# Output projection of a hybrid attention and Hyena layer: left half of the columns for all tokens, then the right half token group by token group

## The chip, the cores and the metric

One core of one Trainium2 chip runs the kernel. The metric is the device time of one execution in microseconds (us), here the median of three runs. The trace comes from one more, profiled execution; its span is counted from its first recorded instruction, and every time below is in us from there.

The engines go by the trace's names: PE is TensorE with its matmuls, ACT is ScalarE, DVE is VectorE, POOL is GpSimd, and SP is the queue that issues most transfers. Each engine works through its own list of instructions in order; an instruction that waits holds up all that stand behind it on that engine.

## What is computed

One layer: attention and a long convolution run side by side, are merged by gates into `y`, and go through one output projection `w_out` (1024 by 1024) into a gated residual. A norm, a router over 64 experts, the experts and a shared expert follow.

```python
def merge_branches(attn_out, hy_out, gate, w_ba, w_bh, w_out):
    ga, gh = jnp.split(gate, 2, axis=-1)
    y = jax.nn.sigmoid(ga) * (attn_out @ w_ba) + jax.nn.sigmoid(gh) * (hy_out @ w_bh)
    return y @ w_out
...
        x_mixed = x + mod[:, 2] * merge_branches(attn, hy_out, gate, w_branch_attn[i],
                                                 w_branch_hyena[i], w_out[i])
...
        x = x_mixed
        h2 = modulate(rmsnorm(x, norm_ffn[i]), mod[:, 3], mod[:, 4])
        x = x + mod[:, 5] * moe(h2, w_router[i], router_bias[i], w_exp_gate[i], w_exp_up[i],
                                w_exp_down[i], w_sh_gate[i], w_sh_up[i], w_sh_down[i])
    return rmsnorm(x, final_norm)
```

There are 512 tokens, in four groups of 128.

## The kernel before, in words

**Matmuls in pairs.** Every fp32 operand of a large matmul is kept as a pair: `hi`, the value cast to a shorter form, and `lo`, what the cast lost. `split` (L103) makes it from the raw weights: ACT casts `hi` (L105), then DVE, or POOL where the caller says so, subtracts it from the raw value (L106). `mm3` (L97) multiplies two pairs with three matmuls (hi·hi, hi·lo, lo·hi).

**Stages of the middle of the kernel.** Attention and Hyena come first. The merge (L872 to L895, eight steps `j`) multiplies by `wbh` and `wba` and leaves `yT`, the merged activations transposed. Then follows the output projection: `outproj(a2)` (L1038) makes both column halves (n = 0, 1, 512 columns each) of two of the four token groups, with four banks of PSUM, over eight slices `j` of the weights. It is called twice, with a2 = 0 and 1, and each call loads and splits all sixteen weight tiles `wo` of 256 KB again. A raw tile stays in one of 7 buffers ("rwb") until it is split; the pair stays in one of 3 ("wb") until its matmuls are done. For n = 0 the `lo` part is DVE's, for n = 1 POOL's. Into the second call the loads of the shared expert's weights are woven, 8 of `wsgu` (`sg`) and 4 of `wsd` (`sd`), with the same raw buffers and `lo` on POOL. In the trace `wo110` is a2 = 1, n = 1, j = 0, and a raw tile has an `r` in front (`rwo`, `rsg`, `rsd`; a group's line leaves numbers out).

**After the matmuls.** DVE multiplies a bank of PSUM by the gate (`to`, L1055) and adds it to the residual (`xt`, L1056). `norm2(a)` (L1058) is a chain over ACT and DVE: ACT squares and sums `xt` (L1062), ACT makes a root (`rs_s`, L136, with a table load before it), five small operations of DVE refine it (L137 to L141), and DVE makes `h` in two passes (L1064, L1065). `turn2(a)` (L1070) transposes `h` on PE in two halves (`px`); ACT copies each half (`h2T`) and casts it (`sx`), DVE subtracts. `logit2(a)` (L1082) multiplies by the router's weights (`plg`, 16 matmuls per group in the trace) and takes a sigmoid (`score`).

**Order.** The order between the stages is the program's for the pinned parts (matmuls, ACT's copies, the shared expert); a scheduler weaves the rest into each engine's list at build time. Before, groups 0 and 1 are normed, turned and routed between and inside the two calls; groups 2 and 3 are normed after the second. The block behind it multiplies the first half of the tokens for the shared expert (`pgsh`, 24 matmuls), turns and routes groups 2 and 3, multiplies the second half (`pgsh` again), and then runs the router and a loop of 64 experts (`pge`, `pxe`, `pye`).

## Time and profile before

| | us |
|---|---|
| median of three runs | 1380.72 |
| the three runs | 1378.25, 1381.03, 1380.72 |
| the profiled execution | 1378.4 |
| its span | 1376.6 |
| mean granted clock of TensorE in it, as a share of full | 0.971 |

The profiled execution lies 2.3 us under the median and 0.15 us over the fastest run; 1.8 us of it lie outside the span. In the span the merge ends and the output projection begins at 495.9 us, the last matmul of the projection ends at 555.2 us, the second half of the shared expert's first product starts at 577.5 us, and the experts run from 610 us on. A stretch is read by the engine that is busy through it, and where none is, by what ends each engine's waits.

### The profile page before, as it was taken

To read this page: it belongs to the slowest core of one execution; us is meant where nothing else is said; L and a number is where in the kernel's file an instruction comes from. 1 tells how busy PE (TensorE), PEld (TensorE's weight loads), DVE (VectorE), ACT (ScalarE), POOL (GpSimd) and SP (SyncE) were. 2 spreads that over 40 slices of the span, in tenths; PEclk is the share of its full clock that TensorE was granted. 3 is DMA by queue.
4 is the path that set the end of the run, shared out by engine and by line. 5 is a ranking of instruction groups with operands and counts; after the bars stand their busy time and mean duration, and the time that the engine had idled before them with its cause. 6 is when DMAs were issued, how large, how long until landed. Compare 5 with 4: busy or idle time off the path is not lost.

```text
span 1376.6 us, 19781 instructions
## 1 busy us (share of the span) xinstructions
PE 1295.7 (94%) x7074; PEld 1051.8 (76%) x7074; DVE 1068.4 (78%) x1637; ACT 880.6 (64%) x1313; POOL 248.6 (18%) x233
## 2 busy tenths in 40 slices
PE   5999999999999998899999999999999999999970
PEld 3687777777776786778888888888888888888750
DVE  3678678986665549668888898988988898889855
ACT  5565554334664346437777877778877787777851
POOL 0000000002242458320111111111111111111120
PEclk8899999999999999899999999999999999999995
DMA  9433556554212647638999999899999999999944
GB/s 332 187 115 134 180 187 227 180 180 146 86 32 93 213 164 237 254 132 288 335 305 328 337 306 305 282 320 329 321 315 325 321 328 320 312 302 302 322 109 177
DMA packets 77063, 332.80 MB, mean 242 GB/s; under 512 B 13763, under 2 KB 15315, under 8 KB 47524
## 3 DMA queue, kind: packets, MB, share of 16 engines
q1 hardware_dynamic: 63460, 305.19, 61.6%
q0 software_dynamic: 11200, 22.14, 8.5%
q10 hardware_dynamic: 2304, 4.20, 0.8%
q8 instruction: 56, 0.92, 0.3%
q14 instruction: 43, 0.35, 0.1%
HBM read 296.91 MB, written 52.97 MB: 254 GB/s over the span
## 4 chain that ended last, share of the span: by engine, by line
PE 57%; DVE 4%; DMA 3%; issue 1%; ACT 1%; DVEq 0%; POOLq 0%; SPq 0%
PE pge L92 26%; PE pye L92 12%; PE pxe L1174 5%; PE pxe L1175 4%; DMA accd<-Ye,ixe 2%; PE pout L92 2%; PE pbh L92 2%; PE pba L92 2%; DMA accd<-Ys,ixs 1%; PE pgsh L92 1%; PE pte L95 1%; PE pysh L92 1%; PE sle L92 1%; DVE h L1065 0%; PE plg L92 0%
## 5 line engine op out<-in xcount | busy, mean ns | idle before, releaser
L1035 POOL DMA_INDIRECT accd<-Ye,ixe x64 | 106.1, 1658 | 607.1 <-ACT Ye L1034 386.3
L1174 PE MATMUL pxe<-oge,h2h 128*128 128x256 f32 x512 | 133.2, 293 | 0.2 <-DVE XTe00l L106 0.2
L1175 PE MATMUL pxe<-oge,h2l 128*128 128x256 f32 x512 | 128.6, 283 | 0.0
L1175 PEld LDWEIGHTS pxe<-oge,h2l 128*128 128x128 f32 x512 | 97.7, 191 | 3.2
L1174 PEld LDWEIGHTS pxe<-oge,h2h 128*128 128x128 f32 x512 | 97.6, 191 | 3.3 <-issue 0.6
L1034 ACT COPY Ye<-pye 128x1024 f32<-128x1024 f32 x64 | 65.1, 1017 | 9.1 <-PE pye L92 6.0
L779 DVE TENSOR_REDUCE st<-S 128x1 f32<-128x768 f32 x32 | 30.5, 956 | 22.7 <-PE S L92 22.0
L1007 ACT ACTIVATE aae<-pge 128x256 f32<-128x256 f32 x64 | 24.8, 387 | 32.4 <-PE pge L92 31.9
L783 ACT ACTIVATE P<-S,st 128x768 f32<-128x768 f32 x32 | 28.9, 903 | 11.9 <-DVE st L779 9.0
L1155 DVE TENSOR_TENSOR oge<-iot,posm 128x256 fp32r<-128x256 f32 x64 | 23.8, 420 | 13.4 <-PE pxe L1175 13.3
L1008 DVE SCALAR_TENSOR_TENSOR aae<-aae,wge,pge 128x256 f32<-128x256 f32 x64 | 30.5, 477 | 0.4
L800 PE MATMUL pT<-ident,P 128*128 128x128 f32 x192 | 29.9, 278 | 0.4 <-ACT PT L801 0.2
L547 POOL DMA_DIRECT2D modd<-br x16 | 7.9, 496 | 121.5 <-DVE br L546 121.5
L92 PE MATMUL po<-PT,V 128*64 128x256 f32 x192 | 29.1, 389 | 0.0
L800 PEld LDWEIGHTS pT<-ident,P 128*128 128x128 f32 x192 | 21.5, 140 | 7.5 <-issue 3.9
L92 PEld LDWEIGHTS sle<-R,oge 128*64 128x64 f32 x256 | 23.5, 137 | 4.2
L801 DVE COPY PT<-pT 128x384 f32<-128x384 f32 x32 | 17.6, 551 | 11.5 <-PE pT L800 11.4
L801 ACT COPY PT<-pT 128x384 f32<-128x384 f32 x32 | 15.3, 478 | 14.9 <-PE pT L800 14.7
L95 PE MATMUL pte<-ident,aae 128*128 128x128 f32 x128 | 24.4, 272 | 0.0
L311 POOL DMA_DIRECT2D specd<-fX x4 | 2.5, 615 | 120.9 <-DVE rl L301 120.1
L92 PE MATMUL pm<-wm,sc 128*32 128x256 f32 x128 | 13.8, 566 | 11.1 <-DMA wm<-in_wmod_dram 11.0
L92 PE MATMUL pgsh<-shguh,sx 128*128 128x512 f32 x64 | 23.8, 440 | 0.0
(6914 smaller groups left out, 4720.1 us busy)
## 6 DMA issues: line engine op xcount, KB each, us to landing
gu0e<-in_wgu_dram SPq DMA_DIRECT2D x64, 1024.0 KB
gu1e<-in_wgu_dram SPq DMA_DIRECT2D x64, 1024.0 KB
de<-in_wd_dram SPq DMA_DIRECT2D x64, 1024.0 KB
wn<-in_wmod_dram SPq DMA_DIRECT2D x16, 1024.0 KB
wm<-in_wmod_dram SPq DMA_DIRECT2D x16, 512.0 KB
rg<-in_win_dram SPq DMA_DIRECT2D x32, 256.0 KB
rwo<-in_wout_dram SPq DMA_DIRECT2D x32, 256.0 KB
rhy<-in_win_dram SPq DMA_DIRECT2D x24, 256.0 KB
```

Source lines behind the costliest of these rows:

```text
L92: pin(pe.matmul(o, lhsT, rhs, start=start, stop=stop))
L95: pin(pe.transpose(o, i, idn))
L779: dve.tensor_reduce(st[:, 0:1], S[:, 0:NKEY], AX.X, ALU.max, negate=True)
L783: act.activation(P, S[:, 0:NKEY], AF.Exp, bias=st[:, 0:1], accum_out=rsum[a][:, h % 2:h % 2 + 1])
L800: pe.transpose(pT[:, i * 128:(i + 1) * 128], P[:, kt * 128:(kt + 1) * 128], ident)
L801: (dve.tensor_copy if k3 else act.copy)(PT[:, 3 * k3:3 * k3 + 3, aa * 128:(aa + 1) * 128], pT.rearrange("p (k q) -> p k q", k=3))
L1007: pin(act.activation(self.aa, pg[:, 0:FF], AF.Silu))
L1008: dve.scalar_tensor_tensor(self.aa, self.aa, self.wg, pg[:, FF:], ALU.mult, ALU.mult)
L1034: act.copy(Y, py)
L1035: gp.indirect_dma_start(out=accd, out_offset=bass.IndirectOffsetOnAxis(ap=self.ix, axis=0), in_=Y, in_offset=None, compute_op=ALU.add, bou ...
L1174: pe.matmul(o, h2h[:, a, js], oh, start=(a % 2 == 0), stop=False)
L1175: pe.matmul(o, h2l[a][:, js], oh, start=False, stop=(a % 2 == 1))
```

## The change

The projection is cut in two others. `outproj_left` makes the left half of the columns for all four token groups at once, in four banks, with each left weight tile loaded and split once. `outproj_right(a)` makes the right half for one token group from eight pairs that stay in place: three in "wb", five in a new pool with tag "wo", through which the left tiles j >= 3 pass too. There are 16 weight loads in place of 32, 16 casts in place of 32, and 16 subtractions, all on DVE, in place of 16 on DVE and 16 on POOL. The number of matmuls stays. To make room, the raw buffers go from 7 to 5, and the gates `gt` of the merge get a pool of their own that is closed before the new pool opens.

The twelve loads of the shared expert stand in two calls of `shared_load` between the norms; half of the `sg` subtractions are now DVE's. The norms, turns and logits come one token group at a time between the right halves. The lists of all five engines are the same as before up to the merge, and again from the transposes of groups 2 and 3 on.

```diff
@@ -862,10 +862,13 @@
+    gst = ExitStack()
+    gtp = gst.enter_context(tc.tile_pool(name="gt", bufs=3, reuse_waits="tile"))
+
-    def gload(src, shape, name, dst=None, lo_eng=None):
-        raw = gpl.tile(shape, F32, name="r" + name, tag="rwb", bufs=7)
+    def gload(src, shape, name, dst=None, lo_eng=None, pool=None):
+        raw = gpl.tile(shape, F32, name="r" + name, tag="rwb", bufs=5)
         sp.dma_start(raw, src)
-        p = dst or pair(gpl, shape, name, "wb", 3)
+        p = dst or (pair(gpl, shape, name, "wb", 3) if pool is None else pair(pool, shape, name, "wo", 5))
         split(p[0], p[1], raw, lo_eng=lo_eng)
         return p
...
-        gt = gpl.tile([128, 2, T], F32, name=f"gt{j}", tag="gt", bufs=3)
+        gt = gtp.tile([128, 2, T], F32, name=f"gt{j}", tag="gt")
...
+    gst.close()
+    opl = mgs.enter_context(tc.tile_pool(name="op", bufs=1, reuse_waits="tile"))
...
+    def wout_load(n, j):
+        return gload(wout[n, :, j], [128, 512], f"wo{n}{j}", pool=opl if j >= 3 else None)
...
+    def outproj_left():
+
+
+        po = [bank(f"pout{a}0") for a in range(NA)]
         for j in range(8):
...
+            w = wout_load(0, j)
+            for a in range(NA):
+                mm3(po[a], at(yT, slice(None), j, slice(a * 128, a * 128 + 128)), w, j == 0, j == 7)
+            if j >= 2:
+                wo1.append(wout_load(1, j - 2))
+        for j in (6, 7):
+            wo1.append(wout_load(1, j))
+        for a in range(NA):
+            residual(po[a], a, 0)
+
+    def outproj_right(a):
+
+        po = bank(f"pout{a}1")
+        for j in range(8):
+            mm3(po, at(yT, slice(None), j, slice(a * 128, a * 128 + 128)), wo1[j], j == 0, j == 7)
+        residual(po, a, 1)
+
+    def shared_load(js):
+        for j in js:
+            gload(wsgu[:, j], [128, 512], f"sg{j}", at(shgu, slice(None), j), gp if j % 2 else None)
+        for f in range(2):
+            if len(js) == 4 and js[0] == 4:
+                for m in range(2):
                     cs = slice(m * 512, m * 512 + 512)
...
+                    gload(wsd[:, f, cs], [128, 512], f"sd{f}{m}", at(shd, slice(None), f, cs), gp)
...
-    outproj(0)
-    for a in range(2):
-        norm2(a)
-        turn2(a)
-    for a in range(2):
-        logit2(a)
-    outproj(1)
+    outproj_left()
+    outproj_right(0)
+    norm2(0)
+    shared_load(range(0, 4))
+    outproj_right(1)
+    turn2(0)
+    norm2(1)
+    shared_load(range(4, 8))
+    outproj_right(2)
+    logit2(0)
+    turn2(1)
     norm2(2)
+    outproj_right(3)
+    logit2(1)
     norm2(3)
     mgs.close()
     ps_open(ctx, y2=1, pg=2, pt=1)
```

On ACT, at the first norm: before, the sum of squares of group 0 (L1062) stands among the casts of `outproj(1)`, with nine of the shared expert's twelve casts behind it.

```order
L105 CAST wo110h_5251<-rwo110_5249 128x512
L105 CAST wo101h_5267<-rwo101_5265 128x512
L105 CAST shguh_4929<-rsg2_5311 128x512
L105 CAST wo111h_5279<-rwo111_5277 128x512
L1062 ACTIVATE h20_4913,ms20_5141<-xt0_3399 128x1024
L105 CAST wo102h_5295<-rwo102_5293 128x512
L136 ACT_TABLE_LOAD
L136 ACTIVATE rs20_s_5145<-rs20_a_5144 128x1
```

After, the same instruction (L1089) stands behind all twelve casts of the shared expert; `wo17` is the last tile of the right half.

```order
L105 CAST wo17h_5132<-rwo17_5130 128x512
L105 CAST shguh_4936<-rsg5_5275 128x512
L105 CAST shguh_4936<-rsg6_5279 128x512
L105 CAST shguh_4936<-rsg7_5283 128x512
L105 CAST shdh_4935<-rsd00_5287 128x512
L105 CAST shdh_4935<-rsd01_5291 128x512
L105 CAST shdh_4935<-rsd10_5295 128x512
L105 CAST shdh_4935<-rsd11_5299 128x512
L1089 ACTIVATE h20_4920,ms20_5176<-xt0_3399 128x1024
L136 ACT_TABLE_LOAD
L136 ACTIVATE rs20_s_5180<-rs20_a_5179 128x1
```

What moved: nine casts, each of which waits for a load, went ahead of the first norm.

On DVE, where the first finished banks are taken out of PSUM. Before:

```order
L106 TENSOR_TENSOR wo100l_5240<-rwo100_5237,wo100h_5239 128x512
L1055 TENSOR_TENSOR to00_5129<-pout00_4933,modb_4688 128x512
L1056 TENSOR_TENSOR xt0_3399<-to00_5129,xt0_3399 128x512
L1055 TENSOR_TENSOR to01_5132<-pout01_4934,modb_4688 128x512
L1055 TENSOR_TENSOR to10_5135<-pout10_4935,modb_4688 128x512
L1056 TENSOR_TENSOR xt0_3399<-to01_5132,xt0_3399 128x512
L106 TENSOR_TENSOR wo101l_5268<-rwo101_5265,wo101h_5267 128x512
L1056 TENSOR_TENSOR xt1_3400<-to10_5135,xt1_3400 128x512
L1055 TENSOR_TENSOR to11_5138<-pout11_4936,modb_4688 128x512
```

After, with two more banks and the subtractions of `wo17`, `sg4` and `sg6` between them:

```order
L106 TENSOR_TENSOR wo16l_5127<-rwo16_5124,wo16h_5126 128x512
L1049 TENSOR_TENSOR to00_5136<-pout00_4940,modb_4691 128x512
L1049 TENSOR_TENSOR to10_5139<-pout10_4941,modb_4691 128x512
L1050 TENSOR_TENSOR xt0_3399<-to00_5136,xt0_3399 128x512
L106 TENSOR_TENSOR shgul_4938<-rsg4_5271,shguh_4936 128x512
L1050 TENSOR_TENSOR xt1_3400<-to10_5139,xt1_3400 128x512
L1049 TENSOR_TENSOR to20_5142<-pout20_4942,modb_4691 128x512
L106 TENSOR_TENSOR wo17l_5133<-rwo17_5130,wo17h_5132 128x512
L106 TENSOR_TENSOR shgul_4938<-rsg6_5279,shguh_4936 128x512
L1049 TENSOR_TENSOR to30_5145<-pout30_4943,modb_4691 128x512
L1050 TENSOR_TENSOR xt2_3401<-to20_5142,xt2_3401 128x512
```

What moved: the subtractions that free the raw buffers for the last `sd` loads now stand behind a wait for PE's left half.

On PE, at the transposes of group 0 (`px200`, `px201`). Before they stand in the first half of the second call's matmuls:

```order
L92 MATMUL pout20_5233<-wo104h_5351,yTh_4551 128x512
L92 MATMUL pout30_5235<-wo104h_5351,yTh_4551 128x512
L95 MATMUL px200_5160<-ident_67,h20_4913 128x128 x4
L95 MATMUL px201_5168<-ident_67,h20_4913 128x128 x4
L92 MATMUL pout21_5234<-wo113l_5336,yTh_4551 128x512
L92 MATMUL pout21_5234<-wo113h_5335,yTl_4552 128x512
L92 MATMUL pout31_5236<-wo113l_5336,yTh_4551 128x512
L92 MATMUL pout31_5236<-wo113h_5335,yTl_4552 128x512
L92 MATMUL pout20_5233<-wo104l_5352,yTh_4551 128x512
L92 MATMUL pout20_5233<-wo104h_5351,yTl_4552 128x512
```

After they stand five matmuls ahead of the projection's end, and group 1's right behind it:

```order
L92 MATMUL pout31_5377<-wo16h_5126,yTh_4554 128x512
L95 MATMUL px200_5239<-ident_67,h20_4920 128x128 x4
L95 MATMUL px201_5247<-ident_67,h20_4920 128x128 x4
L92 MATMUL pout31_5377<-wo16l_5127,yTh_4554 128x512
L92 MATMUL pout31_5377<-wo16h_5126,yTl_4555 128x512
L92 MATMUL pout31_5377<-wo17h_5132,yTh_4554 128x512
L92 MATMUL pout31_5377<-wo17l_5133,yTh_4554 128x512
L92 MATMUL pout31_5377<-wo17h_5132,yTl_4555 128x512
L92 MATMUL plg0_5331<-wrt_4927,h2T0_5236 128x64 x8
L95 MATMUL px210_5345<-ident_67,h21_4921 128x128 x4
L92 MATMUL plg1_5405<-wrt_4927,h2T1_5342 128x64 x4
L95 MATMUL px211_5353<-ident_67,h21_4921 128x128 x4
```

What moved: the transposes and logits of groups 0 and 1 went from the inside of the projection to its end.

## Rows read from the trace of the kernel before

**Rows 1.** The page: the chain that ended last, shares of the span.

```profile
PE pge L92 26%; PE pye L92 12%; PE pxe L1174 5%; PE pxe L1175 4%; DMA accd<-Ye,ixe 2%; PE pout L92 2%; PE pbh L92 2%; PE pba L92 2%; DMA accd<-Ys,ixs 1%; PE pgsh L92 1%; PE pte L95 1%; PE pysh L92 1%; PE sle L92 1%; DVE h L1065 0%; PE plg L92 0%
```

**Rows 2.** Busy time by stretch of the span (us from its start), core 0.

```profile
core 0: us, PE busy (x) PEld busy (x) DVE busy (x) ACT busy (x) POOL busy (x), PEclk, DMA share, GB/s
...
517.40:540.60 23.20, 19.66 (x91) 14.28 (x89) 22.86 (x29) 16.04 (x30) 18.99 (x12) 1.00 0.79 256
...
495.70:577.50 81.80, 70.68 (x325) 56.34 (x324) 58.32 (x80) 47.49 (x82) 52.68 (x34) 0.94 0.62 213
720.00:1240.00 520.00, 520.00 (x2828) 441.92 (x2827) 460.21 (x605) 412.98 (x529) 77.42 (x47) 1.00 0.94 316
```

**Rows 3.** TensorE's waits, 495 to 620 us: what for, us in total, times, longest.

```profile
PE px L95 <- DVE rs_r L137: 3.1, 2, 2.4
PE px L95 <- DVE h L1065: 2.3, 1, 2.3
...
PE plg L92 <- ACT score L1086: 1.3, 1, 1.3
```

**Rows 4.** The chain of work that ended last, 495 to 620 us: start, length, what.

```profile
495.89 18.59 PE pout L92 x82
...
549.47 1.73 PE plg L92 x16
...
574.17 3.58 PE plg L92 x16
577.75 4.45 PE pgsh L92 x12
...
582.42 2.81 PE pgsh L92 x12
```

**Rows 5.** TensorE in order of time: start, length, instruction (idle before and its releaser).

```profile
577.51 0.77 PE L92 MATMUL pgsh<-shguh,sx 128*128 128x512 f32 x1
```

**Rows 6.** VectorE, the same view.

```profile
515.79 1.77 DVE L106 TENSOR_TENSOR wo100l<-rwo,wo100h 128x512 fp32r<-128x512 f32 x1
...
518.20 0.69 DVE L1056 TENSOR_TENSOR xt<-to,xt 128x512 f32<-128x512 f32 x1
...
524.65 0.68 DVE L1055 TENSOR_TENSOR to<-pout,modb 128x512 f32<-128x512 f32 x1
...
559.72 0.17 DVE L137 RECIPROCAL rs_r<-rs_s 128x1 f32<-128x1 f32 x1 [0.76 <-ACT rs_s L136]
...
560.69 1.28 DVE L1064 SCALAR_TENSOR_TENSOR h<-xt,rs_r,modb 128x1024 f32<-128x1024 f32 x1
...
563.15 0.16 DVE L137 RECIPROCAL rs_r<-rs_s 128x1 f32<-128x1 f32 x1
...
565.43 1.23 DVE L1065 TENSOR_TENSOR h<-h,modb 128x1024 f32<-128x1024 f32 x1
```

**Rows 7.** ScalarE, the same view.

```profile
459.66 0.62 ACT L105 CAST wa2h<-rwa 128x512 fp32r<-128x512 f32 x1 [2.20 <-PE pbh L92]
...
513.33 0.62 ACT L105 CAST shguh<-rsg 128x512 fp32r<-128x512 f32 x1 [1.77 <-DMA rsg<-in_wsgu_dram]
...
530.41 0.62 ACT L105 CAST shdh<-rsd 128x512 fp32r<-128x512 f32 x1 [0.66 <-DMA rsd<-in_wsd_dram]
...
557.01 1.07 ACT L1062 ACTIVATE h<-xt 128x1024 f32<-128x1024 f32 x1 [5.16 <-DVE xt L1056]
```

**Rows 8.** GpSimd, the same view.

```profile
498.35 1.29 POOL L106 TENSOR_TENSOR wo011l<-rwo,wo011h 128x512 fp32r<-128x512 f32 x1
...
520.74 1.73 POOL L106 TENSOR_TENSOR wo110l<-rwo,wo110h 128x512 fp32r<-128x512 f32 x1
```

**Rows 9.** SyncE, issuing the loads, the same view.

```profile
452.10 0.33 SPq L867 DMA_DIRECT2D rwa<-in_wba_dram  x1
...
510.23 0.33 SPq L867 DMA_DIRECT2D rsg<-in_wsgu_dram  x1
...
525.90 0.33 SPq L867 DMA_DIRECT2D rsd<-in_wsd_dram  x1
```

More of the change, by code (lines that the diff above doesn't have):

```diff
@@ L1036, in emit @@
                                   in_offset=None, compute_op=ALU.add, bounds_check=T - 1, oob_is_err=False)
-    def outproj(a2):
-        po = {(a, n): bank(f"pout{a}{n}") for a in (2 * a2, 2 * a2 + 1) for n in range(2)}
-        for j in range(8):
-            for n in range(2):
-                w = gload(wout[n, :, j], [128, 512], f"wo{a2}{n}{j}", lo_eng=gp if n else None)
-                if a2 == 1 and n == 1:
-                    gload(wsgu[:, j], [128, 512], f"sg{j}", at(shgu, slice(None), j), gp)
-                if a2 == 1 and n == 0 and j >= 4:
-                    f, m = divmod(j - 4, 2)
-                    cs = slice(m * 512, m * 512 + 512)
-                    gload(wsd[:, f, cs], [128, 512], f"sd{j}", at(shd, slice(None), f, cs), gp)
-                for a in (2 * a2, 2 * a2 + 1):
-                    mm3(po[a, n], at(yT, slice(None), j, slice(a * 128, a * 128 + 128)), w, j == 0, j == 7)
-        for a, n in po:
-            cs = slice(n * 512, n * 512 + 512)
-            t = gpl.tile([128, 512], F32, name=f"to{a}{n}", tag="to")
-            dve.tensor_tensor(t, po[a, n], modb[:, MG, cs], ALU.mult)
-            dve.tensor_tensor(xt[a][:, cs], t, xt[a][:, cs], ALU.add)
@@ new lines, in wout_load, with residual @@
+    def wout_load(n, j):
+        return gload(wout[n, :, j], [128, 512], f"wo{n}{j}", pool=opl if j >= 3 else None)
+    def residual(po, a, n):
+        cs = slice(n * 512, n * 512 + 512)
+        t = gpl.tile([128, 512], F32, name=f"to{a}{n}", tag="to")
+        dve.tensor_tensor(t, po, modb[:, MG, cs], ALU.mult)
+        dve.tensor_tensor(xt[a][:, cs], t, xt[a][:, cs], ALU.add)
+    wo1 = []
+    def outproj_left():
+        po = [bank(f"pout{a}0") for a in range(NA)]
+        for j in range(8):
+            w = wout_load(0, j)
[7 more added lines that the diff above has]
+            residual(po[a], a, 0)
```

## The prediction, on record before the changed kernel ran

> **What bounds the kernel now.** I begin with the chain of work that ended last, to see which stage sets the end. The experts' matmuls hold the largest shares of it (26%, 12%, 5% and 4%), the output projection only 2% [rows 1]. The busy times by stretch say how the two hang together: from 720 to 1240 us TensorE is busy 520.00 of 520.00 us at full clock [rows 2]. The experts are a block of fixed length that starts when what comes ahead of it is done. So a microsecond won or lost before the experts moves the end by one, unless their loads then set the pace; the DMA share of 0.94 in the same row keeps that open.
>
> Second, the stretch that is rewritten, from 495.7 us to the second half of the shared expert's product at 577.5: there TensorE is busy 70.68 of 81.80 us, VectorE 58.32, ScalarE 47.49, GpSimd 52.68 [rows 2]. No engine is full, so the waits tell more than the shares. TensorE waits for `h` and the root behind it before the transposes (2.3 and 3.1 us) and for `score` (1.3 us) [rows 3]. These are links of the norm chain. After some of these gaps the clock is low: 16 router matmuls take 3.58 us after the last one against 1.73 earlier, 12 of the shared expert 4.45 against 2.81 [rows 4]. The question is how early the fourth norm can end, and what follows it.
>
> **What falls away.** 16 loads, 16 casts and 16 subtractions. No matmul goes. 82 matmuls of the projection take 18.59 us on the chain [rows 4], 0.227 each, so the loads and splits were only partly in the way, and their removal by itself is worth the few waits on split weights. The larger part of the gain must come from the norms: before, the last two groups are normed only after all matmuls; now their left halves are done early and only the right half of the last group is late.
>
> **The merge with five raw buffers.** One load that waited for a buffer went out at 452.10 [rows 9]; with two buffers fewer the two loads issued ahead of it join it. The earlier of them, `wa2`, was cast at 459.66 [rows 7]. Even 4.5 us of loading, the longest below, leaves 3 us. I cost this at nothing; if several of these loads came late it would cost 1 to 2 us once. I keep the start at 495.9.
>
> **The left half.** 99 matmuls (96, and 3 of the right half that stand among them) by 0.227 are 22.5 us: the end is at 518.2. The weights come faster than they are used (one tile feeds 12 matmuls in place of 6), so I add no wait.
>
> **From there to the first norm.** This is the new wait. ScalarE's sum of squares for group 0 stands behind all twelve casts of the shared weights. The last, `sd11`, needs a raw buffer that VectorE frees with the subtraction of `sg6`, and this stands behind the first banks (`to`), which wait for the left half. From 518.2 VectorE has three `to` from PSUM at 0.68 and five operations that read only SBUF. Alone these take 0.69, beside GpSimd's subtractions 1.77 [rows 6]. So `sg6` is done between 518.2+2.0+3.5 = 523.7 and 518.2+2.0+8.9 = 529.1. GpSimd is at work for about half of this (its subtractions of `sg5`, `sg7` and `sd00`, 1.29 to 1.73 each [rows 8]); I take 526.4. Then the load: from issue to cast 3.1 us for one (510.23 to 513.33) and 4.5 for another (525.90 to 530.41) [rows 7, 9]. I take 4.5, since that one ran in the stretch with a DMA share of 0.79 [rows 2]. With the cast, 0.62, the sum of squares starts at 531.5. Earliest: `sg6` at 523.7 and a load of 3.1 give 527.4, but group 0's right half itself is only in `xt` at about 528 (TensorE: 18+14+2 matmuls after 518.2, then `to` and `xt`). Latest: 529.1+4.5+0.6 = 534.2.
>
> What the rows show of this sharing is that VectorE's subtraction grows by 1.08 us and GpSimd's by 0.44, and that `to` stays at 0.68 [rows 6, 8]. The Trainium skill (SBUF — State Buffer, section "Who interferes with whom") speaks of an exclusive lock: VectorE operations with two SBUF inputs are shut out while GpSimd holds the shared port. Three GpSimd subtractions would then shut VectorE out for 3.9 us in place of the 2.7 in my sum, and the gain would be 1.2 us smaller. That `to` is spared agrees with the page; that GpSimd's operations grow too means that both take turns, and I keep the rows.
>
> **The norm chain.** From the sum of squares to the end of `h` it was 557.01 to 563.15 [rows 6, 7], 6.1 us: `h` of group 0 at 537.6. TensorE reaches this group's transposes at about 538.9 (88 right-half matmuls after 518.2, and half a us for `wo17`), so they wait for nothing. From here VectorE is the bound. Group 1: five small operations 0.97 (559.72 to 560.69), `to` and `xt` of group 2 1.4, two passes for `h` 2.46 (560.69 to 563.15) [rows 6]: 542.4. Group 2: again 0.97 and 2.46, two `sx` and one `to` at 0.68 (all read PSUM), one small operation 0.2, `xt` of group 3 0.69: 548.8. With that the fourth norm may start: 6.1, and 0.2 for a `score` between: 555.1. Before, the fourth `h` ended at 566.66 (565.43+1.23) [rows 6], so this link comes 11.5 us earlier.
>
> **Behind the fourth norm.** From there the lists are the same instructions in the same order, and the second half of the shared product started at 577.51 [rows 5], 10.85 us later. What may be late is its first half, which before was done long before. It now follows the logits of group 1, at about 547.5; its 24 matmuls take 5.6 us at the speed of 2.81 for 12 and 8.9 at that of 4.45 [rows 4], so it ends between 553 and 556.4 and costs 0 to 1.5 us. I take 0.5. Should the low clock not come back, the last router matmuls and the product behind them win (3.58-1.73)+(4.45-2.81) = 3.5 us more. I assume it comes back, as TensorE still waits there for `score`.
>
> **The sum.** 11.5-0.5 = 11.0 us, so the execution of 1378.4 becomes 1367.4. That execution was 2.3 below the median of the runs; against the median it is 1369.7. I say **1368.5**. Ends of this case: the latest sum of squares (2.7 later) and 1 us more for the product give 7.3, or 1371 to 1373.5; the earliest (3.5 earlier) 15.0, or 1363.4 to 1365.7.
>
> **Rivals.** *The ring keeps up and the clock stays*: the casts are done when `xt` is, gain 14 to 18, 1360 to 1366. For it speaks that one weight tile feeds twice the matmuls, so all loads start earlier; against it the place of the casts, behind two waits. Chance 0.17.
> *The ring is slow, but not so slow*: loads of 6 to 8 us when 28 tiles pass 5 buffers, and a gain of 3 to 7, 1372 to 1377. Chance 0.08.
> *The experts take it back*: if their loads and not TensorE set the pace, an earlier start only waits later; 1378 to 1380. For it the DMA share of 0.94, against it TensorE's 520.00 of 520.00. Chance 0.08.
> *Slower*: the same ring, ahead of the norm. Three loads stand in each other's way (`sg2` takes the buffer of `sg0`, `sg5` that of `sg2`, `sd01` that of `sg5`), and each has to land, be cast and subtracted. Every us on a turn costs three. The gain is gone when the sum of squares starts 11 us later, at 542.5, which takes 4 us more per turn, a landing of 8 us and over; at 545 the time is 1383. The rows show 3.1 to 4.5. Chance 0.06.
> My forecast has the rest, 0.61.
>
> **How the numbers follow.** A measurement tells about 0.2%, 2.8 us, from no change. Faster by more: the forecast, the first rival and the second, 0.61+0.17+0.08, less a little for the second's upper edge: 0.85. Within: 0.09. Slower: 0.06. The range reaches over the first rival's better half and the slow ring, from 1361 to 1377; outside lie the experts' giving back, the slower case and the edge of the first.
>
> **What would show it.** Right: twelve shared casts directly ahead of the first sum of squares, and this at 531 (528 to 534); `h` of the fourth group near 555; the second half of the shared product near 566; experts unchanged in length. Wrong: TensorE waiting within the left half (the weight loads too late); the sum of squares after 536 (the ring); the first half of the shared product ending after 557 (clock); an experts' block that is longer by what was won.

## The result, and the profile after

The changed kernel takes **1362.38 us** (median of four runs, 1361.62 to 1364.24) against 1379.81 for the kernel before, measured beside it (four runs, 1378.25 to 1381.03). The ratio is 0.9882 with a 95% interval of 0.9864 to 0.9900. The profiled execution took 1361.81 us with a span of 1360.0, 16.6 less than the 1376.6 of before; mean granted clock 0.977.

The page of the changed kernel, the chain that ended last, shares of the span (answers to [rows 1]). The experts' shares are those of before, within 1%:

```profile
PE pge L92 26%; PE pye L92 13%; PE pg L92 7%; PE phy L92 5%; PE pxe L1207 5%; PE pxe L1208 4%; PE pout L92 3%; PE S L92 2%; PE pn L92 2%; PE po L92 2%; DMA accd<-Ye,ixe 2%; PE pq L92 2%; PE pbh L92 2%; PE pba L92 2%; PE pT L800 2%; PE p L92 1%
```

Busy time by stretch, the columns as in [rows 2]. The first line is the rewritten stretch, the second and third are the projection and what follows the fourth norm:

```profile
core 0: us, PE busy (x) PEld busy (x) DVE busy (x) ACT busy (x) POOL busy (x), PEclk, DMA share, GB/s
495.40:577.50 82.10, 78.45 (x392) 65.03 (x391) 61.20 (x139) 41.72 (x72) 22.52 (x14) 1.00 0.59 222
...
495.50:540.20 44.70, 44.70 (x204) 37.05 (x203) 32.29 (x57) 23.07 (x41) 13.03 (x10) 1.00 0.54 184
...
552.00:566.00 14.00, 11.70 (x76) 9.82 (x74) 8.36 (x12) 10.51 (x17) 9.49 (x4) 1.00 0.96 380
```

The same two stretches in the kernel before, its projection and the time from the fourth norm to the second half of the shared product:

```profile
495.70:555.40 59.70, 53.34 (x242) 42.01 (x241) 42.34 (x51) 34.55 (x61) 43.58 (x29) 0.97 0.61 200
...
567.50:582.00 14.50, 12.18 (x58) 10.27 (x57) 7.54 (x15) 8.10 (x14) 9.48 (x4) 0.76 1.02 403
```

The projection is the place. It lasts 44.7 us in place of 59.7, and TensorE is busy in all of it, where before 6.4 us were idle. Not all of the difference is won: 40 of the matmuls that stood in it before (32 of the router, 8 transposes) now follow it, where they take 4.9 us (1.73, 0.46, 1.10, 0.46 and 1.10). GpSimd's busy time in it falls from 43.58 to 13.03 us and ScalarE's from 34.55 to 23.07; a large part of this is the 16 splits that are gone, the rest has moved behind it or to VectorE. Behind the fourth norm the clock is now full (1.00 against 0.76).

TensorE's waits from 440 to 620 us (answers to [rows 3]; the four lines that are left out are links of the experts', the attention's and the merge's parts):

```profile
PE plg L92 <- ACT h2T L1104: 1.4, 2, 0.7
PE plg L92 <- ACT score L1113: 1.3, 1, 1.3
PE px L95 <- DVE sx L1107: 1.0, 2, 0.7
```

No `px` waits for a norm any more. The chain from 490 to 600 us (answers to [rows 4]: start, length, what):

```profile
495.72 42.44 PE pout L92 x187
...
540.19 1.73 PE plg L92 x16
...
561.04 2.00 PE plg L92 x16
563.03 2.86 PE pgsh L92 x12
```

The projection stands on the chain as one unbroken piece of 187 matmuls, 0.227 each, the price of [rows 4]. After the last wait for `score` the router's 16 matmuls take 2.00 and twelve of the shared product 2.86, where [rows 4] had 3.58 and 4.45.

VectorE in order of time, the subtraction and residual adds ahead of the first norms, and the end of the fourth `h` (answers to [rows 6]):

```profile
521.55 1.43 DVE L106 TENSOR_TENSOR wo17l<-rwo,wo17h 128x512 fp32r<-128x512 f32 x1
522.91 0.68 DVE L106 TENSOR_TENSOR shgul<-rsg,shguh 128x512 fp32r<-128x512 f32 x1
...
524.11 2.89 DVE L1050 TENSOR_TENSOR xt<-to,xt 128x512 f32<-128x512 f32 x2
...
527.63 1.07 DVE L1050 TENSOR_TENSOR xt<-to,xt 128x512 f32<-128x512 f32 x1
...
550.69 1.23 DVE L1092 TENSOR_TENSOR h<-h,modb 128x1024 f32<-128x1024 f32 x1
```

ScalarE, the last casts of the shared weights, and the sums of squares of the first and the fourth group (answers to [rows 7]):

```profile
526.14 1.88 ACT L105 CAST shdh<-rsd 128x512 fp32r<-128x512 f32 x3 [1.64 <-DMA rsd<-in_wsd_dram]
528.74 1.07 ACT L1089 ACTIVATE h<-xt 128x1024 f32<-128x1024 f32 x1 [0.72 <-DVE xt L1050]
...
545.58 1.07 ACT L1089 ACTIVATE h<-xt 128x1024 f32<-128x1024 f32 x1
```

The line at 528.74 decides a question of the prediction: the first sum of squares waited 0.72 us for `xt`, not for the casts ahead of it, which were done at 528.02. VectorE, which writes `xt`, had no idle time from 517.95 to 528.70: its `to` of this group's right half began at 526.92, behind two stretched `xt`, though TensorE's last matmul for it ended at 526.14.

GpSimd's subtractions beside these VectorE rows (answers to [rows 8]):

```profile
521.14 1.30 POOL L106 TENSOR_TENSOR shgul<-rsg,shguh 128x512 fp32r<-128x512 f32 x1 [1.94 <-ACT shguh L105]
523.22 1.52 POOL L106 TENSOR_TENSOR shgul<-rsg,shguh 128x512 fp32r<-128x512 f32 x1 [0.79 <-ACT shguh L105]
524.71 1.74 POOL L106 TENSOR_TENSOR shdl<-rsd,shdh 128x512 fp32r<-128x512 f32 x1
```

**Where the 16.6 us of the span come from.** The projection ends 15.2 us earlier (540.18 against 555.36). From its end to the end of the fourth `h` it is 11.7 us, before 11.3, so 0.4 are lost. From there to the last 16 router matmuls it is 9.1 us, before 7.5, so 1.6 are lost. The full clock gives back 1.6 in these 16 matmuls and 1.6 in the twelve behind them. From the experts' first matmul to the end it is 765.5 us, before 765.9. Together 15.2-0.4-1.6+3.2+0.4 = 16.8, which is the 16.6 to within 0.2.

### The profile page after: what moved, and what is told of

It reads as the page before. It is cut to its first block, busy times and chain, and to the rows that moved or that the text cites. A ratio compares the mean times of both kernels' runs of the same rounds, so it can differ in the third digit from the quotient of the medians.

```text
span 1360.0 us, 19693 instructions
## 1 busy us (share of the span) xinstructions
PE 1285.6 (95%) x7074; PEld 1046.0 (77%) x7074; DVE 1058.1 (78%) x1641; ACT 871.7 (64%) x1297; POOL 215.3 (16%) x213
## 4 chain that ended last, share of the span: by engine, by line
PE 88%; DMA 4%; DVE 3%; ACT 3%; issue 1%; SPq 0%; DVEq 0%; POOLq 0%; ACTq 0%
PE pge L92 26%; PE pye L92 13%; PE pg L92 7%; PE phy L92 5%; PE pxe L1207 5%; PE pxe L1208 4%; PE pout L92 3%; PE S L92 2%; PE pn L92 2%; PE po L92 2%; DMA accd<-Ye,ixe 2%; PE pq L92 2%; PE pbh L92 2%; PE pba L92 2%; PE pT L800 2%; PE p L92 1%
## 5 line engine op out<-in xcount | busy, mean ns | idle before, releaser
L1188 DVE TENSOR_TENSOR oge<-iot,posm 128x256 fp32r<-128x256 f32 x64 | 23.9, 419 | 13.4 <-PE pxe L1208 13.3
L92 PE MATMUL sle<-R,oge 128*64 128x4 f32 x256 | 23.6, 189 | 0.0
L95 PEld LDWEIGHTS pte<-ident,aae 128*128 128x128 f32 x128 | 17.5, 139 | 7.2
```

Source lines behind the costliest of these rows:

```text
L92: pin(pe.matmul(o, lhsT, rhs, start=start, stop=stop))
L95: pin(pe.transpose(o, i, idn))
```

## The experiments

The theory after the result was: what is saved (16 loads, casts, subtractions) and the new order work together, because ScalarE and VectorE carry the splits and the norms in the same queues. The rivals: the saved work alone does it; the order alone does it; the clock does it.

The profiles of all kernels are compared by four marks. The start of the projection differs by up to 4 us between executions (last experiment), so the other three are counted from it: the first sum of squares, the end of the fourth `h`, and the first transpose of the shared expert behind twelve matmuls of the product's second half ("product"). Each profile is of one execution. Those of a_best and a_reload_dve lie 4.5 and 3.1 us under the median of their runs, that of a_dvelo 2.2 over it, and that of b_fill is its slowest run (1387.80), with a longer experts' part. The kernel before was run again beside each group of kernels (medians 1378.86 to 1380.27); the ratios are taken beside these, and give differences between kernels that are up to 2 us smaller than those of the medians, which the text uses.

| kernel | time, us (lowest to highest) | ratio to before, 95% | start | sum of squares | fourth `h` | product |
|---|---|---|---|---|---|---|
| before | 1379.81 (1378.25–1381.03) | 1 | 495.7 | 26.4 | 70.9 | 86.3 |
| after | 1362.38 (1361.62–1364.24) | 0.9882 (0.9864–0.9900) | 495.6 | 33.2 | 56.4 | 70.2 |
| b_noload | 1370.31 (1368.35–1371.10) | 0.9928 (0.9898–0.9957) | 495.8 | 27.8 | 61.4 | 78.6 |
| b_noload_late | 1369.01 (1367.36–1371.41) | 0.9924 (0.9899–0.9949) | 497.2 | 27.5 | 61.7 | 75.4 |
| a_reload | 1377.47 (1375.98–1380.07) | 0.9979 (0.9964–0.9995) | 495.9 | 36.5 | 65.9 | 84.6 |
| a_reload_dve | 1377.59 (1374.51–1379.72) | 0.9981 (0.9959–1.0003) | 495.4 | 38.1 | 68.2 | 82.7 |
| a_ring3 | 1374.37 (1371.36–1377.18) | 0.9955 (0.9937–0.9973) | 498.0 | 36.0 | 65.2 | 80.6 |
| a_dvelo | 1370.84 (1369.19–1373.06) | 0.9929 (0.9905–0.9952) | 499.0 | 35.7 | 59.6 | 76.6 |
| b_fill | 1381.81 (1379.26–1387.80) | 1.0026 (1.0008–1.0044) | 495.1 | 26.5 | 70.8 | 87.9 |
| a_gap | 1371.56 (1370.13–1374.02) | 0.9947 (0.9927–0.9968) | 495.3 | 33.6 | 56.5 | 78.0 |
| a_onebank | 1362.55 (1361.69–1364.08) | 0.9876 (0.9853–0.9899) | 496.1 | 33.6 | 56.7 | 69.0 |
| a_best | 1364.40 (1359.83–1366.67) | 0.9881 (0.9854–0.9909) | 494.4 | 33.5 | 54.3 | 69.2 |

### The saved work alone: b_noload

The kernel before, whose second call takes weights of the first call that are still there, so nothing is loaded or split a second time.

```diff
-                w = gload(wout[n, :, j], [128, 512], f"wo{a2}{n}{j}", lo_eng=gp if n else None)
+                if a2 == 0:
+                    w = gload(wout[n, :, j], [128, 512], f"wo{a2}{n}{j}", lo_eng=gp if n else None)
+                    lastw.append(w)
+                else:
+                    w = lastw[-3:][(2 * j + n) % 3]
```

> The kernel before, with the sixteen loads, casts and subtractions of the second call left out; the second call multiplies with three pairs that the first call left in place, so the projection of groups 2 and 3 is not the reference's. This is the change's saving of work alone, in the old order. Theory (two parts: TensorE no longer waits for weights inside the projection, and the logits and a transpose of groups 0 and 1 move under the fourth norm): only the first part is here. The projection took 59.3 us for 192 matmuls x 0.227 = 43.6 and 5.9 of transposes and logits; the 9.9 us above that are waits and low clock. They shrink to 0 to 2.5, the projection ends at 545.5 to 548, the fourth h follows 11.5 us later, and the time falls by 7 to 10: 1370 to 1373. Rival 1 (the saved work is the whole gain): 1362 to 1364. Rival 2 (the saved work was hidden, order is all): 1378 to 1380.

Measured 1370.31, as the theory said: about 9.9 us under before, and so about three fifths of the whole gain (by the ratios 0.72 of 1.18%). The projection lasts 49.9 us in place of 59.6. Its waits on split weights, 3.2 us in four places before, are gone, and of the waits for norms one of 1.3 is left. From 525 us to its end the clock is 1.00; before, it was 0.93 from 530 us on. So the removal won three times the waits that it took away. A part of the rest is seen on VectorE and GpSimd of the kernel before, in order of time, at the root of the second norm, which stands on the chain there:

```profile
535.62 1.25 DVE L138 TENSOR_TENSOR rs_s<-rs_r 128x1 f32<-128x1 f32 x1
536.90 1.20 DVE L139 TENSOR_TENSOR rs_s<-rs_s,rs_a 128x1 f32<-128x1 f32 x1
...
538.33 1.02 DVE L141 TENSOR_TENSOR rs_r<-rs_r,rs_s 128x1 f32<-128x1 f32 x1
```
```profile
535.11 1.74 POOL L106 TENSOR_TENSOR wo114l<-rwo,wo114h 128x512 fp32r<-128x512 f32 x1
536.82 1.27 POOL L106 TENSOR_TENSOR shgul<-rsg,shguh 128x512 fp32r<-128x512 f32 x1
538.05 1.28 POOL L106 TENSOR_TENSOR shdl<-rsd,shdh 128x512 fp32r<-128x512 f32 x1
```

The three VectorE operations took 0.16 each at the fourth norm, where GpSimd was idle. Here each ended within 0.02 us of the subtraction that GpSimd was at when it began (536.87 and 536.85, 538.10 and 538.09, 539.35 and 539.33). I estimate from the rows, each against its length without GpSimd beside it, that VectorE's operations on two SBUF operands were longer by about 16 us in all from 495 to 556 us before, by 8 in b_noload and by 4 in the changed kernel. So GpSimd's subtractions held up VectorE, and with it the norms, beyond TensorE's waits for their results. How much of the 9.9 us is this, and how much the shorter lists, no run separates.

The chain and the router's matmuls say what was not won:

```profile
547.44 1.15 ACT h L1068 x2
...
555.90 1.24 DVE h L1071
...
565.67 3.67 PE plg L92 x16
569.34 5.21 PE pgsh L92 x12
```

Two norms still follow the projection's end at 545.6, the fourth `h` comes 11.5 us after it, and the low clock behind it is still there. So the saved work shortens the projection. That it is 5.3 us shorter still in the changed kernel is mostly the 40 matmuls that moved behind it. What the changed kernel has over b_noload are a fourth `h` that is 5.0 us earlier and, with the full clock behind it, a product mark that is 8.4 earlier.

### Half of the work given back in the new order: a_reload, a_reload_dve

The changed kernel; the right weights are loaded and split once more for groups 2 and 3 (eight splits, half of what the change saves), with the subtractions on GpSimd or, in the second kernel, on VectorE.

```diff
     shared_load(range(4, 8))
+    wo1[:] = [gload(wout[1, :, j], [128, 512], f"wr1{j}", lo_eng=gp, pool=opl if j >= 3 else None) for j in range(8)]
     outproj_right(2)
```

(a_reload_dve is the same line without `lo_eng=gp`.)

> The changed kernel with the eight right-hand weight tiles loaded, cast and subtracted (on GpSimd) a second time for groups 2 and 3: half of the saved work is put back, the rest of the new order stays. The schedule that results multiplies groups 2 and 3 together. Theory: TensorE does not wait for the loads (they land while the first two right halves run), but group 2's norm comes as late as group 3's: fourth h 1 to 3 us later, 1363.5 to 1366. Rival 1 (the saved work is the gain): half of the gain back, 1370 to 1372.

Measured 1377.47: 15 of 17.4 us are gone (by the ratios 13.4 of 16.3), far outside both expectations. GpSimd and TensorE of a_reload, in order of time:

```profile
527.64 4.21 POOL L106 TENSOR_TENSOR shdl<-rsd,shdh 128x512 fp32r<-128x512 f32 x3 [0.52 <-DMA rsd<-in_wsd_dram]
531.80 1.27 POOL L106 TENSOR_TENSOR wr10l<-rwr,wr10h 128x512 fp32r<-128x512 f32 x1
```
```profile
529.83 0.73 PE L92 MATMUL pout<-wr10h,yTh 128*128 128x512 f32 x2 [1.04 <-ACT wr10h L105]
533.13 0.79 PE L92 MATMUL pout<-wr10l,yTh 128*128 128x512 f32 x1 [2.56 <-POOL wr10l L106]
```

The first new subtraction stands behind three of the shared weights on GpSimd, and TensorE waits 3.6 us for the first pair. The `x2` of the first row says more: the same tile is multiplied for two groups in turn. The build put groups 2 and 3 together, so that both are left to norm at the end, and the order of the change is not kept in this run. The fourth `h` is 9.6 us later than in the changed kernel, and the piece behind it is 4.9 longer, with `px` waiting 2.9 for `sx` and the low clock back (16 router matmuls 3.67).

To see whether the GpSimd queue is the cause, the second kernel moves the subtractions.

> As a_reload (right-hand weights loaded and split a second time for groups 2 and 3), but with the second subtractions on VectorE, where a_reload had them on GpSimd behind four of the shared weights' subtractions. There TensorE waited 3.6 us for the first reloaded tile and its clock fell behind that wait, and the projection ended at 550.9 in place of 540.2. Theory (a_reload lost its gain to GpSimd's queue and the low clock behind it, not to the loads): TensorE's wait falls to 0 to 1.5 us, the projection ends at 540 to 544, 1363 to 1368. Rival (second loads cost their time wherever they are split): 1375 to 1378.

TensorE's waits for weights shrink to 2.2 us and the projection lasts 47.5 in place of 55.0, as the theory said, yet the time is the same, 1377.59, as its rival said. ScalarE of a_reload_dve:

```profile
532.97 0.62 ACT L105 CAST wr13h<-rwr 128x512 fp32r<-128x512 f32 x1 [1.27 <-DMA rwr<-in_wout_dram]
533.50 1.06 ACT L1089 ACTIVATE h<-xt 128x1024 f32<-128x1024 f32 x1
...
537.18 0.62 ACT L105 CAST wr16h<-rwr 128x512 fp32r<-128x512 f32 x1 [0.97 <-DMA rwr<-in_wout_dram]
537.71 1.06 ACT L1089 ACTIVATE h<-xt 128x1024 f32<-128x1024 f32 x1
```

The sums of squares of the first two norms stand behind casts that wait for loads (the first starts 4.9 us later than in the changed kernel), and the last two norms end together, 20.7 us after the projection (11.7 in the changed kernel). So the splits hurt less through TensorE's waits for weights than through the norms. Two causes lie in this, the splits in the norms' queues and groups 2 and 3 multiplied together, and these runs don't part them. With half of the saved work given back, the kernel is 0.2% faster than before; what the order of the change is worth without the saved work was not measured.

### The order without the norms in between: b_noload_late

b_noload, with the turns and logits of groups 0 and 1 behind the second call, so that nothing of the norms stands between its matmuls.

```diff
+    outproj(1)
+    for a in range(2):
         turn2(a)
...
         logit2(a)
-    outproj(1)
     norm2(2)
```

> The kernel before without the second call's loads, casts and subtractions (as in b_noload: the second call multiplies with three pairs left by the first, so groups 2 and 3 are not the reference's), and with the transposes and logits of groups 0 and 1 placed behind the whole projection, as the change does. In b_noload the projection ended at 545.6 and the fourth h 11.5 us later. Theory (the gain has two parts that add: no waits for weights, and the transposes and logits of groups 0 and 1 run under the fourth norm): the projection ends 5 to 6 us earlier, at 539.5 to 541, the fourth h near 552, and the time is that of the changed kernel, 1361 to 1364, without its split by columns. Rival (the second part needs the norms token group by token group): as b_noload, 1368 to 1371.

The projection is 5 us shorter than in b_noload (44.9), as expected, since transposes and logits now stand behind it, but the time is the same, 1369.01, as the rival said. VectorE in order of time:

```profile
554.15 2.47 DVE L1070 SCALAR_TENSOR_TENSOR h<-xt,rs_r,modb 128x1024 f32<-128x1024 f32 x2
556.54 2.35 DVE L1071 TENSOR_TENSOR h<-h,modb 128x1024 f32<-128x1024 f32 x2
```

Groups 2 and 3 are normed at once, after the turns and two `score` with their table loads, and the fourth `h` ends 61.7 us after the start, as in b_noload. A shorter projection is worth nothing by itself. What counts is where the fourth norm ends. With transposes and logits behind the matmuls, the fourth `h` ends 16.8 us after them when two groups are left to norm, as here, and 11.7 when one is left, as in the changed kernel. That one is what the column halves give.

### The ring of raw buffers: a_ring3

```diff
-        raw = gpl.tile(shape, F32, name="r" + name, tag="rwb", bufs=5)
+        raw = gpl.tile(shape, F32, name="r" + name, tag="rwb", bufs=3)
```

> The changed kernel with 3 raw buffers in place of 5, nothing else. In the trace of the changed kernel the last shared cast ended at 528.02 and the first sum of squares started at 528.74 when xt was written, so the ring had 0.7 us to spare. Theory: with three buffers 28 loads of 3 to 4.5 us with cast and subtraction (4.5 to 6 us a turn for 3 tiles) take 42 to 56 us from 478 on; the last cast comes at 531 to 540 and the first sum of squares 2 to 11 us later; the time is 1364 to 1374. Rival (the prediction's slower case): over 1380. Rival (the ring has much more to spare than the trace shows): 1361 to 1363.

Measured 1374.37, 12 us slower than with five, at the upper end of what the theory gave; the last cast, at 544.59, is later than its 531 to 540. ScalarE in order of time:

```profile
544.59 0.62 ACT L105 CAST shdh<-rsd 128x512 fp32r<-128x512 f32 x1 [1.96 <-DMA rsd<-in_wsd_dram]
545.11 1.05 ACT L1089 ACTIVATE h<-xt 128x1024 f32<-128x1024 f32 x1
...
556.23 1.07 ACT L1089 ACTIVATE h<-xt 128x1024 f32<-128x1024 f32 x1
```

The casts of the shared weights now reach into the third norm, and the fourth stands behind the turns. The prediction's mechanism of the ring is real; with five buffers it is just paid, with 0.7 us to spare (528.02 against 528.74).

### No subtraction on GpSimd: a_dvelo

```diff
-            gload(wsgu[:, j], [128, 512], f"sg{j}", at(shgu, slice(None), j), gp if j % 2 else None)
+            gload(wsgu[:, j], [128, 512], f"sg{j}", at(shgu, slice(None), j), None)
...
-                    gload(wsd[:, f, cs], [128, 512], f"sd{f}{m}", at(shd, slice(None), f, cs), gp)
+                    gload(wsd[:, f, cs], [128, 512], f"sd{f}{m}", at(shd, slice(None), f, cs), None)
```

> The changed kernel with all twelve subtractions of the shared weights on VectorE, GpSimd idle there: 8 more on VectorE. In the trace of the changed kernel VectorE's SBUF-only operations between 518 and 532 were lengthened by some 4 us in all while GpSimd subtracted. Theory (sharing costs about what the subtraction costs): 8 x 0.69 = 5.5 us more work against 4 us less stretching, the first sum of squares 0 to 2.5 us later, 1362 to 1365. Rival (sharing is the dearer): first sum of squares earlier, 1360.5 to 1362.

Measured 1370.84, slower by 8 (4 in the single runs of the last experiment), which neither the theory nor its rival gave. No VectorE operation is stretched there, but eight more subtractions stand ahead of `xt`, the first sum of squares is 2.5 us later, groups 0 and 1 are normed together, and the fourth `h` is 3.3 later; another 3.1 are lost behind it, where the clock falls once more (the twelve product matmuls ahead of the mark take 4.40 in place of 2.86). In this kernel sharing SBUF with GpSimd costs less than doing its work.

### The wait and the clock behind the fourth norm: b_fill, a_gap

b_fill puts ten matmuls that nobody reads ahead of the third group's transposes in the kernel before:

```diff
     shared[0].gateup()
+    pf = bank("pfill", tag="pt")
+    for i in range(10):
+        mm(pf, sx[0][0][:, 0:128], shgu[0][:, i % 8], i == 0, i == 9)
     halve2(0)
```

> The kernel before, with 10 matmuls (128x512) into a bank that nobody reads, placed ahead of the transposes of group 2, where TensorE waits 2.43 us for h: 10 x 0.23 = 2.3 us, so the wait is filled and nothing is made later. Theory of the clock (after waits of this size the low clock stretches the router matmuls to 3.58 and the next twelve of the shared expert to 4.45 us, against 2.00 and 2.86 in the changed kernel): with the wait filled these two fall to about 2.0 and 2.9 and the time falls by 2 to 3.3 us, 1376.5 to 1378. Rival (the low clock there has nothing to do with this wait): both stay at 3.6 and 4.4, time 1379.5 to 1380.5.

The theory fell: 1381.81 beside 1378.86 for the kernel before. TensorE in order of time:

```profile
559.85 2.50 PE L92 MATMUL pfill<-shguh,sx 128*128 128x512 f32 x10
562.64 1.07 PE L95 MATMUL px<-ident,h 128*128 128x128 f32 x8 [0.29 <-DVE rs_r L137]
568.76 0.78 PE L95 MATMUL px<-ident,h 128*128 128x128 f32 x4 [2.25 <-DVE sx L1080]
...
570.64 3.52 PE L92 MATMUL plg<-wrt,h2T 128*128 128x64 f32 x16
```

The ten filled the wait for the norm (2.4 before, 0.29 here), but TensorE then waited 2.25 at the next link, and the clock fell there. Here the work put into one gap, of a chain that another engine sets, only moved the gap.

a_gap goes the other way: in the changed kernel the last twelve matmuls of the product's first half, which stand between the norms' transposes, go behind the last logits.

```diff
-    shared[1].gateup(0, 4)
     turn2(3)
...
     logit2(3)
+    shared[1].gateup(0, 4)
     shared[1].gateup(4, 8)
```

> The changed kernel with the first twelve matmuls of the shared product of group 1 moved from between the transposes of groups 2 and 3 to behind the logits: the same work, but TensorE is idle some 3 us more before the last logits. Theory of the clock: the twelve matmuls add 2.8 us behind the fourth norm, and the longer idle time lets the clock fall as in the kernel before, which adds up to 1.6+1.6 us on the last logits and the first matmuls, and as much as 2.8 us on the moved ones: 1367 to 1370. Rival (clock does not fall): 2.8 us, 1365.

Measured 1371.56, 9 us slower and a little more than the theory's 1367 to 1370, though the fourth `h` is where it was (56.5). TensorE of a_gap and then of the changed kernel, the same instructions:

```profile
556.28 0.71 PE L95 MATMUL px<-ident,h 128*128 128x128 f32 x4 [3.62 <-DVE sx L1107]
...
561.99 3.67 PE L92 MATMUL plg<-wrt,h2T 128*128 128x64 f32 x16 [0.31 <-ACT score L1113]
```
```profile
556.36 0.66 PE L95 MATMUL px<-ident,h 128*128 128x128 f32 x4 [0.67 <-DVE sx L1107]
...
561.04 2.00 PE L92 MATMUL plg<-wrt,h2T 128*128 128x64 f32 x16 [1.31 <-ACT score L1113]
```

The transposes start at the same time. Behind the longer wait the clock fell, the second half starts 2.6 us later, and the 24 matmuls then take 7.95 us where twelve took 2.90, of which 2.8 are the moved ones: 4.8 us of the 7.6 by which the product mark is later in this stretch are the clock's. So a part of the measured gain is that this stretch is now filled.

### Can more be had: a_onebank, a_best

a_onebank puts the logits of groups 2 and 3 into one bank with one `score` for both; a_best does so for all four groups and also places all norms ahead of the turns of groups 0 and 1.

```diff
-    logit2(2)
-    logit2(3)
+    logit2_pair(2)
```

> The changed kernel with the logits of groups 2 and 3 in one bank and one sigmoid for both, nothing else. In the trace TensorE waited 1.31 us there for the score of group 2, behind a table load. Theory: the 1.31 us and about 0.3 of the second score are gone, 1360.5 to 1361.5. Rival (the sigmoid's table load is then on the path in its place): 1362 to 1363.

> The changed kernel with the norms ahead of the transposes: norm 0 to 3 follow their right halves, the transposes and logits of groups 0 and 1 come after; the logits of two groups share one bank and one sigmoid, so that no logit matmul waits for a score; one operation adds the bias for all groups. The same work. In the trace of the changed kernel the projection ended at 540.0, but the last xt was written at 545.2 and the fourth sum of squares began at 545.6. Theory: the last xt is written at 541 to 542, the fourth h ends at 548 to 550 in place of 551.9, the router matmuls lose a wait of 1.3 us; together 3 to 5 us less, 1357.5 to 1359.5. Rival (what follows the fourth h is set by TensorE's own list, 24+12 matmuls of the shared expert and the transposes): 1 us or less, 1361.5 to 1362.5.

Measured 1362.55 and 1364.40. For a_onebank that is its rival's figure; a_best is slower than both of its expectations, with two of six runs at 1359.9 and four at 1364.0 to 1366.7. Its profile is of one of the two. Both kernels take away the wait of 1.3 us for `score`. In the profiles the fourth `h` of a_best is 2.0 us earlier and the product mark of both 1.0 to 1.2 earlier. In time neither can be told from the changed kernel (0.9876 and 0.9881 against 0.9882). Half of the 2 us of the norms doesn't reach the product: TensorE is then busy with its own list (12.00 of 12.00 us from 552 to 564 in a_best), so the bound behind the norms has changed. I found no version that is measurably faster than the changed kernel.

### The same kernels again: a_again, a_dvelo_again

No edit; the changed kernel and a_dvelo once more, one execution each.

> The changed kernel once more, unaltered, for its start of the output projection, which in the profiles so far lay between 494.4 and 499.0 us though the lists up to there are nearly the same. If this start belongs to the single execution, it may come anywhere in 494 to 499 here, and times of links have to be taken from the start of the projection. If it belongs to the kernel (where its tiles lie, what its early loads meet), it is 495.6 again, within 0.4. The links counted from the start stay in either case: the projection's end 44.6 later, the fourth h 56.4, the second half of the shared product about 67.3; time 1361 to 1365.

> The kernel with all twelve shared subtractions on VectorE once more, unaltered. Its projection began at 499.0 in the first profile, 3.4 later than in the changed kernel. If the start belongs to the execution, 494 to 499; if it belongs to the kernel, 499.0 again within 0.4, and then 3.4 of its 8 us are no price of the norms. Counted from the start of the projection the first sum of squares stands at 35.7 and the fourth h at 59.6 in either case; time 1369 to 1373.

The start belongs to the execution: a_dvelo began its projection at 499.0 and now at 494.9, and its links counted from there stayed (first sum of squares 35.7 both times, fourth `h` 59.6 and 59.7). Its time is now 1367.65, under the expected 1369 to 1373, still 4 us over the changed kernel's 1363.59 beside it. The changed kernel began at 495.4; its fourth `h` is 57.3 from there (1 later than in the first profile) and the product mark 72.4 (2.2 later). Busy time from 548 to 552 us, a_again first, then the first profile of the changed kernel:

```profile
548.00:552.00 4.00, 4.00 (x10) 3.04 (x10) 2.57 (x7) 1.18 (x2) 0.00 (x0) 0.50 0.14 53
```
```profile
548.00:552.00 4.00, 4.00 (x20) 3.17 (x19) 3.39 (x8) 0.37 (x3) 0.00 (x0) 1.00 0.00 0
```

Here one execution had half the clock and one the full, in the same piece of the shared product (10 matmuls against 20 in 4 us), after waits of at most 0.9 and 0.7 us. So differences of 1 to 2 us at the product mark say nothing (those of a_onebank and a_best among them), and the sum above belongs to one execution. The full clock behind the last `score` is there in both.

## Why the prediction was right or wrong

The forecast was 1368.5; the result is 1362.38, inside the range by 1.4 us. The gain was 11 us predicted and 16.6 measured in the same terms. The direction was right, and so was the chain of the norms as the thing that sets the time. But two conditions of the forecast, the ring as the bound of the first norm and the low clock behind the fourth, did not come true: what came true is the first rival (the ring keeps up, the clock stays, gain 14 to 18), to which I had given 0.17.

- **The merge and the left half: right.** The start was kept (495.7 and 495.6). The left half ended at 518.2, as predicted (the prediction's own sum, 495.9+22.5, is 518.4), and no weight was waited for.
- **From there to the first norm: too late by 2.8 us.** Predicted 531.5, measured 528.74. The `sg6` subtraction was done at 523.6, the early end of the bound, as only one of VectorE's operations ahead of it was stretched; I had taken the middle. With the load at 4.5 us this made the ring the bound. In fact the bound was `xt` of group 0, which the prediction had at "about 528" as its earliest case. The trace also decides between the two pictures of sharing. `wo17l` began at 521.55 beside a subtraction of GpSimd that ran to 522.44, and took until 522.98: it stood until GpSimd was done. GpSimd's next began at 523.22, while VectorE was at `sg6` (to 523.59), and took 1.52. In the two `xt` (2.89) and GpSimd's 1.74 beside them each waited for the other in turn. This agrees with the exclusive lock of the Trainium skill (SBUF — State Buffer, section "Who interferes with whom"): whichever of the two comes second is shut out until the first is done. The prediction took it as a sign against the lock that GpSimd's operations grow too; that reading was wrong, since either engine can be the second.
- **The norm chain: right within 0.7 us.** From the sum of squares to `h` 6.1 predicted and 6.35 measured; from the first `h` to the fourth 17.5 and 16.8. The fourth `h` ended at 551.9, predicted 555.1.
- **The tail: too cheap by 1.1.** 0.5 us predicted for the product's first half and its neighbours; the piece from the fourth `h` to the last logits grew by 1.6.
- **The clock: the wrong side.** I let it fall again and named 3.5 us for the other case. It stayed, which gave 3.2 us. The rows on which I had relied showed a wait for `score` there, and this wait is still there (1.31), so it does not bring the low clock by itself. In a_gap the clock fell behind a longer wait ahead of the logits, 3.62 against 0.67. What brought it down in the kernel before stays open: the three waits next to it there were 0.69, 0.32 and 1.32, as now (0.67, 0.31 and 1.31), and a wait of 2.43 stood further ahead, after which the clock was 0.52 (564 to 566 us), then 1.00 (568 to 574) and low again behind `score` (0.58 from 574 to 576). b_fill took the wait of 2.43 away, and the low clock came all the same.
- **The claim on the saved work: wrong.** I wrote that the removal of loads and splits is worth only the few waits on split weights, and the larger part must come from the norms. These waits were 3.2 us; b_noload, which removes the work alone, gained 9.9. The step that failed was to price a queue by the waits of TensorE on its own results: ScalarE and VectorE had the splits in the same lists as the norms, and GpSimd's splits stretched VectorE's operations. TensorE's waits for the norms, behind which the clock fell too, hung on this.
- **The rivals.** The experts did not take it back: 765.9 us before and 765.5 after, and 764 to 767 in all but one of the other profiles (b_fill, 774.3). The slow ring did not come with five buffers, and a_ring3 shows that it comes with three. The weights are split once, as the change says.

In sum: 3.2 us earlier norms, 3.2 for the clock, 1.1 back for the tail and 0.3 of small change are the 5.6 by which 11.0 became 16.6.

## What to carry to other kernels

Price work that is taken off a queue not only by who waits for its result, but by everything that stands behind it in that queue: here sixteen splits cost 10 us while the waits on their results were about 3, and eight put back in another order, which also changed the order of the matmuls, cost 15. Look too at what the operations of another engine do to that queue: VectorE's were some 16 us longer beside GpSimd's. When a chain of norms follows a block of matmuls, cut the block so that only one group is left at its end, and judge an edit by where the last link ends and not by how long the block lasts: here a matmul block that was 5 us shorter was worth nothing, and a gap filled ahead of the last link came back at the next.

## What the runs showed of the hardware

- The start of one and the same stretch varied between 494.4 and 499.0 us from execution to execution, with the same kernel too (499.0 and 494.9). Profiles that differ by a few us have to be lined up at a stage's start before links are compared.
- The granted clock after short waits isn't fixed by the program: with waits of 0.7 us and 0.9 us ahead of it, 4 us of the same matmuls ran at 1.00 in one execution and at 0.50 in another. After waits of 2.1 to 3.6 us at the transposes of the last two groups (before, b_noload, b_fill, a_gap, a_reload) the last 16 router matmuls took 3.6 to 3.7 us; in the kernel before the 16 ahead of them, nearer to that wait, took 1.9. Where no wait there was over 1.4 (after, a_again, a_dvelo, a_dvelo_again, a_reload_dve, b_noload_late, a_ring3) they took 2.0 to 2.7. But in four of these (a_dvelo, a_dvelo_again, b_noload_late, a_ring3) the clock fell there, and the next twelve matmuls took 3.8 to 4.4 in place of 2.9. What decides it is open.
- VectorE's operations on two SBUF operands that began while GpSimd subtracted ended only after it: operations of 0.16 us took up to 1.25, and ones of 0.69 up to 1.79. Where VectorE was first, GpSimd's grew from 1.28 to as much as 2.26. VectorE's `to`, one operand of which is in PSUM (0.68), and its RECIPROCAL, which reads one operand (0.15), kept their length beside GpSimd.
